# One latent trunk layer on one core: own tiles for each context head, two more weight pairs, and a new order of the opening

## The chip, the cores and the metric

The kernel runs on one core of one Trainium2 chip. The metric is the device time of one execution in microseconds; of several runs the median is taken. Matrix products are made on TensorE (PE), elementwise work on VectorE (DVE), ScalarE (ACT) and GpSimd (POOL); SyncE (SP) issues nearly all transfers.

## The reference, cut to what matters

One layer over 2048 latent rows (`x`) and 256 context rows (`ctx`), 1024 wide. The parts that the opening of the kernel computes:

```python
ada   = silu(c) @ w_ada + b_ada            # shifts and scales for x
ada_c = silu(c_ctx) @ w_ada + b_ada        # shifts and scales for the context
hc = modulate(rmsnorm(xc, norm_mix[l]), csh1, csc1)
logf_f, k_f, logf_b, k_b, vc = hgrn2_gates(hc @ w_in[l][:, :3 * w], lb_f, lb_b, first)
hf_c = advance_state(h0, k_f, vc, jnp.cumsum(logf_f, axis=2))
hb_c = advance_state(h0, flip_t(k_b), flip_t(vc), jnp.cumsum(flip_t(logf_b), axis=2))
h = modulate(rmsnorm(x, norm_mix[l]), sh1, sc1)
o, _, _ = token_mixers(h @ w_in[l], lb_f, lb_b, first, hf_c, hb_c, *mix_args)
x = x + g1 * (o @ w_out[l])
```

`hc @ w_in` has 3 x 512 columns: four heads with a forward gate, a backward gate and a value column block of 128 each, so 12 blocks. `hf_c` and `hb_c` are one 128 x 128 state per head and direction, from which the latent scans start. Then come a second normalisation, a gated MLP with a 3 x 3 convolution, and a last norm.

## The kernel before, in words

All large products are made as three products of split operands: `split` (L129) rounds an array to a high part on ScalarE (L131, a cast) and subtracts it to get the low part on VectorE or GpSimd (L132); `mm3` and `run_banks` multiply high by high, high by low and low by high into one PSUM bank. A *column* here is one block of 128 columns of `w_in` (its first column number is its key: 0 and 128 ... for the forward gates, 512 ... for the backward gates, 1024 ... for values, 2048 for the output gate of head 0). A *bank* is the product of one column with 256 context rows or with 512 rows of x: 24 matrix products.

**The opening**, L332 to L390, is written in a fixed order. `load_ada` fetches four 512-column groups of the conditioning weights. Groups 0, 2 and 3 are multiplied on TensorE (`ada_products`); group 1 is summed on VectorE (`ada_sums`, L290) and added up over the partitions by eight small products per sequence with a column of ones (`ada_ones`, L293). `ctx_mod` (L308) applies shift and scale to the context, block by block, and splits it; `ctx_products` (L323) starts the first column. `x_square` (L229) sums the squares of a tile of 128 rows on ScalarE, `rstd` makes the factors on GpSimd, `x_scale` (L234) multiplies a tile by them on VectorE (L238).

**The banks** behind it are the list `seq` (L1043 to L1047), an order written by hand in a string: `c` is the next of the 12 context banks, `g` a bank of head 0's output gate on x (the two share the column 2048), `v` and `q` its value and query banks, `s` and `t` banks of the gating unit. `run_banks` (L512) makes each bank, and before it fetches and splits the columns of the next two. A split column lies in one of two operand pairs (`w_free`, L209); it gives the pair back when its last bank is done. Raw columns come through three buffers.

Between banks `slot` steps two queues of background work. `bg_q` holds `x_start` (L406: normalise and transpose the first 1024 rows of x; `x_first` modulates and splits them, L243 and L132, into `xh` and `xl`; odd blocks get the low part on VectorE, even ones on GpSimd), then `misc`, then `x_second` (the other 1024 rows, to memory). `hg_q` holds `ctx_state` (L599) of each context head: seven level updates of the keys (L501) with products of totals (L508) on VectorE, four transposes, four products. The context heads share two sets of tiles in turn (`sets`, L638), so head h waits for the state of head h - 2 (L649).

A scheduler then orders the instructions on each engine, except in the fixed part and for those that are pinned.

Of the kernel before, what the change touches and what calls it, by code (L numbers as in the profile page):

```python
# [18 lines left out]
P = 128  # L19
# [64 lines left out]
def tile_trunk(ctx, tc, x, c, cx, c_ctx, w_ada, b_ada, norm_mix, norm_ffn, w_in, hg_norm, sgu_g, sgu_b,  # L84
# [104 lines left out]
    with es1:  # L189
# [18 lines left out]

        w_n, w_raw, w_free = [0], {}, [0, 1]  # L209

# [5 lines left out]
        def split_w(key, eng=None):  # L216
            if key not in w_raw:
                load_raw(key)
            raw, at = w_raw.pop(key), w_free.pop(0)
            hi = p1.tile([P, NK, P], F32R, tag=f"whi{at}", name="whi", align_bytes=AL)  # L220
            lo = p1.tile([P, NK, P], F32R, tag=f"wlo{at}", name="wlo", align_bytes=AL)
            w_n[0] += 1
            split(hi, lo, raw, eng or (V if w_n[0] < 8 or w_n[0] < 20 and w_n[0] % 2 else G))
            return hi, lo, at

        def x_sums():
            return pm.tile([P, 8], F32, tag="xss", name="xss", bufs=2)
# [6 lines left out]
        def x_scale(xs, ss, keep=pin):  # L234

            r = rstd(pm, ss[:, :len(xs)], len(xs), 1.0 / D, keep=keep)
            for i, xt in enumerate(xs):
                keep(V.tensor_scalar(out=xt, in0=xt, scalar1=r[:, i:i + 1], scalar2=None, op0=ALU.mult))  # L238

# [83 lines left out]
        def ctx_products(c, ks):  # L323
            hi, lo, _ = nxt[c, CTX]
            pj = opened[c, CTX]
            for k in ks:
                mm3(pj[:, :CTX], hi[:, k, :], lo[:, k, :], chl[:, k, :], cll[:, k, :], k == 0, False)

# [3 lines left out]
        with tc.manual_schedule():  # L332
# [33 lines left out]
            ada_rows(0, "ot")  # L366
            ada_sums(1, 0, 5)
            load_raw((2 * HW, CTX))
# [4 lines left out]
            ada_products(3, 1, 8)  # L373
            ctx_mod(0)
            ada_sums(1, 5, 8)
            for k in range(1, 4):
                ctx_mod(k)
                ada_sums(0, k - 1, k)
            nxt[HW, CTX] = split_w((HW, CTX), V)
            ss0 = x_sums()  # L380
            x_square(xg[:1], ss0, keep=lambda i: i)
            ada_rows(3, "ot")
            ada_ones(1, small, 256)
            ada_columns(3)
# [7 lines left out]
        xh = p1.tile([P, NK, TH], F32R, tag="xh", name="xh", align_bytes=AL)  # L392

# [12 lines left out]
        def x_start():  # L406
            xk = [pk.tile([P, 2, D], F32, tag="K", name="xk", bufs=2, align_bytes=AL) for i in range(2)]
            xs = [xk[i // 2][:, i % 2, :] for i in range(4)]
            ss, ss2 = ss0, x_sums()
            for q in range(2):  # L410
                x_square(xg[2 * q + 1:2 * q + 3], ss, 2 * q + 1)
                for i in range(2 * q, 2 * q + 2):
                    pin(ld(xs[i], x_rows[4 + i]))
                if q:
                    x_scale(xg, ss)
                yield 2.0
            for i, w in enumerate(x_first(0, xg)):
# [38 lines left out]
        def misc():  # L456

            for l in range(0, 8, 4):
                mf = pm.tile([P, 4, P], F32, tag="gu", name="mf", bufs=2)
                ld(mf, masks.rearrange("p (l j) -> p l j", j=P)[:, l:l + 4, :])  # L460
                V.tensor_copy(msk[:, l:l + 4, :], mf)
            yield 1.0
            wsr = pm.tile([P, NH, P], F32, tag="nt", name="wsr", bufs=2)
            ld(wsr, w_sp[0].rearrange("h p q -> p h q"))
# [47 lines left out]
        def run_banks(banks, peek=None):  # L512
# [3 lines left out]
            for i, (col, n0, n, sink, pre) in enumerate(banks):  # L516
                if pre is not None:
                    pre()
                up = list(dict.fromkeys(keys[i:] + tail))
                for key in up[:2]:  # L520
                    if key not in nxt:
                        nxt[key] = split_w(key)
# [4 lines left out]
                pj = opened.pop(keys[i], None)  # L527
                k0 = 0 if pj is None else 4
                pj = pj or bank("pj")
# [68 lines left out]

        def ctx_state(h, F, K, vt):  # L599
            tot = F  # L600
            for B in LV:
# [29 lines left out]
        def marked(g, what):  # L631
# [12 lines left out]
        for h in range(NH):  # L644
            F, K, vt = sets[h % 2]

            def pre(h=h):
                if h >= 2:
                    need(hg_q, ("ctx", h - 2))  # L649
                if h:  # L650
                    F, K, vt = sets[(h - 1) % 2]
                    hg_q.add(marked(ctx_state(h - 1, F, K, vt), ("ctx", h - 1)))
# [5 lines left out]
        def ctx_last():  # L658
            hg_q.add(marked(ctx_state(NH - 1, *sets[1]), ("ctx", NH - 1)))

# [1145 lines left out]
```

## Time and profile before

| | us |
|---|---|
| median of 3 runs | 2476.84 (2475.95 to 2477.19) |
| the profiled execution | 2477.96 |
| its span, first to last instruction | 2476.2 |
| TensorE busy (share of the span) | 2421.4 (98%) |
| VectorE, GpSimd, ScalarE busy | 1784.7 (72%), 1053.7 (43%), 968.2 (39%) |

The span is what the profile shows; the profiled execution's own time is 1.8 us longer and lies 1.1 us above the median. Times in the rows are counted from the start of the span. A row's bracket tells how long the engine was idle before it and what ended that.

### The profile page before, as it was taken

The page shows a single profiled execution, that of the slowest core. Times are in us where ns is not written, and L with a number is a line of the kernel's source. Part 1 is how long each engine was busy: PE and PEld are TensorE (multiplying, and loading weights), DVE is VectorE, ACT ScalarE, POOL GpSimd, SP SyncE. Part 2 cuts the span into 40 slices and gives each one's busy share as a digit, 9 for nine tenths or more (in the row PEclk, how much of TensorE's full clock was granted, in tenths as well). Part 3 has the DMA queues.
Part 4 walks back from the last instruction along what each step waited for, and adds up shares of the span by engine and source line. Part 5 has one row for each costly group of instructions (what it writes and reads, how often), then busy time and mean ns, then how long its engine had stood idle before and what let it go on. Part 6 is the DMA issues. An engine that isn't in the chain of part 4 may idle for free.

```text
span 2476.2 us, 32805 instructions
## 1 busy us (share of the span) xinstructions
PE 2421.4 (98%) x11859; PEld 2009.7 (81%) x11859; DVE 1784.7 (72%) x2374; ACT 968.2 (39%) x1614; POOL 1053.7 (43%) x866
## 2 busy tenths in 40 slices
PE   7899999999999999999999999999999999999998
PEld 4787888788888888788878888888878888888887
DVE  5766875645765866465699778759999993776876
ACT  3454334434344443244443333334333342432343
POOL 1344232332333433100588787887878770000002
PEclk9999999999999999999999999999999999999999
DMA  8365445573353422768932222472222239834645
GB/s 304 96 191 184 128 137 189 177 261 120 103 182 129 144 99 86 241 210 258 310 106 90 89 80 90 143 273 86 83 93 85 91 101 354 309 120 153 225 149 195
DMA packets 307854, 400.12 MB, mean 162 GB/s; under 512 B 33113, under 2 KB 216161, under 8 KB 304621
## 3 DMA queue, kind: packets, MB, share of 16 engines
q1 hardware_dynamic: 304404, 397.28, 48.3%
q8 instruction: 94, 1.54, 0.3%
q10 hardware_dynamic: 3289, 0.76, 0.1%
q14 instruction: 67, 0.55, 0.1%
HBM read 288.85 MB, written 109.13 MB: 161 GB/s over the span
## 4 chain that ended last, share of the span: by engine, by line
PE 37%; DVE 7%; issue 3%; POOL 2%; ACT 1%; DMA 1%; SPq 0%; POOLq 0%; ACTq 0%; DVEq 0%
PE up L65 23%; PE dn L65 14%; DVE dn L1373 3%; DVE edges L1378 1%; DVE gp L1454 1%; ACT dn L1370 1%; POOL Al L132 0%; DMA yd<-fl 0%; POOL ra L1665 0%; POOL rr L1666 0%; DVE keep L1448 0%; POOL raw L1191 0%; DVE keep L1464 0%; ACT Ah L131 0%; ACT cv L1392 0%
## 5 line engine op out<-in xcount | busy, mean ns | idle before, releaser
L1373 DVE SCALAR_TENSOR_TENSOR dn<-gp,taps,dn 128x1024 f32<-128x1024 f32 x352 | 448.6, 1281 | 21.1 <-ACT dn L1370 17.9
L65 PE MATMUL up<-yf,Ah 128*128 128x512 f32 x1232 | 393.5, 389 | 0.0
L65 PE MATMUL dn<-thl,mhl 128*128 128x512 f32 x1680 | 381.5, 389 | 1.2 <-ACT thl L131 1.2
L132 POOL TENSOR_TENSOR Al<-raw,Ah 128x512 fp32r<-128x512 f32 x264 | 343.0, 1308 | 89.5 <-ACT Ah L131 81.4
L65 PEld LDWEIGHTS dn<-thl,mhl 128*128 128x128 f32 x1680 | 315.0, 188 | 67.7 <-ACT thl L131 2.0
L65 PE MATMUL pj<-xh,whi 128*128 128x512 f32 x896 | 363.8, 406 | 0.0
L65 PE MATMUL pj<-xh,wlo 128*128 128x512 f32 x896 | 350.8, 392 | 1.2 <-DVE wlo L132 1.2
L65 PE MATMUL pj<-xl,whi 128*128 128x512 f32 x896 | 350.3, 391 | 1.2 <-POOL xl L132 1.0
L65 PE MATMUL up<-xah,Al 128*128 128x512 f32 x704 | 275.5, 391 | 3.4 <-POOL Al L132 3.1
L65 PE MATMUL up<-xah,Ah 128*128 128x512 f32 x704 | 274.6, 390 | 0.6 <-ACT Ah L131 0.6
L65 PEld LDWEIGHTS up<-yf,Ah 128*128 128x128 f32 x1232 | 231.2, 188 | 47.9
L131 ACT CAST Ah<-raw 128x512 fp32r<-128x512 f32 x264 | 160.6, 618 | 276.3 <-PE up L65 213.7
L132 POOL TENSOR_TENSOR wlo<-raw,whi 128x1024 fp32r<-128x1024 f32 x55 | 135.5, 2464 | 250.3 <-ACT whi L131 224.3
L65 PE MATMUL up<-xal,Ah 128*128 128x512 f32 x528 | 205.5, 389 | 0.0
L65 PE MATMUL up<-yf,Al 128*128 128x512 f32 x528 | 205.2, 389 | 0.0
L65 PEld LDWEIGHTS pj<-xh,wlo 128*128 128x128 f32 x896 | 168.3, 188 | 37.5 <-DVE wlo L132 1.7
L65 PEld LDWEIGHTS pj<-xh,whi 128*128 128x128 f32 x896 | 168.8, 188 | 32.8 <-issue 3.5
L65 PEld LDWEIGHTS pj<-xl,whi 128*128 128x128 f32 x896 | 168.9, 189 | 31.8 <-POOL xl L132 1.8
L65 PE MATMUL dn<-wo,o 128*128 128x512 f32 x768 | 182.9, 394 | 1.8 <-DVE nt L706 0.9
L65 PEld LDWEIGHTS dn<-wo,o 128*128 128x128 f32 x768 | 141.9, 188 | 31.7 <-issue 1.1
L65 PEld LDWEIGHTS up<-xah,Al 128*128 128x128 f32 x704 | 132.1, 188 | 36.0 <-POOL Al L132 8.6
L1665 POOL TENSOR_SCALAR ra<-ss 128x1 f32<-128x1 f32 x8 | 5.3, 662 | 359.8 <-ACT jk L1657 359.8
(317 smaller groups left out, 4186.9 us busy)
## 6 DMA issues: line engine op xcount, KB each, us to landing
raw<-in_w_up_dram SPq DMA_DIRECT2D x88, 512.0 KB, 4.5
mr<-m SPq DMA_DIRECT2D x85, 512.0 KB, 5.3
raw<-in_w_in_dram SPq DMA_DIRECT2D x68, 512.0 KB, 4.3
sT<-wd SPq DMA_DIRECT2D x88, 256.0 KB, 4.4
raw<-in_w_ada_dram SPq DMA_DIRECT2D x32, 512.0 KB, 3.9
yf<-yd SPq DMA_DIRECT2D x14, 1024.0 KB
m<-cv SPq DMA_DIRECT2D x22, 544.0 KB, 2.7
raw<-in_w_down_dram SPq DMA_DIRECT2D x22, 512.0 KB, 3.8
```

The lines of the kernel that those rows point to most:

```text
L65: return self.engine.matmul(out, lhsT, rhs, **kw)
L131: keep(S.copy(hi, raw))
L132: (eng or G).tensor_sub(lo, raw, hi.bitcast(F32))
L1370: S.activation(cr, gt[:, 0:RH, 0:GW], AF.Identity, bias=cvb[:, f:f + 1], scale=taps[:, f:f + 1])
L1373: V.scalar_tensor_tensor(out=cr, in0=gt[:, t // 3:t // 3 + RH, t % 3:t % 3 + GW], scalar=taps[:, t * NF + f:t * NF + f + 1], in1=cr, op0=A ...
L1378: V.scalar_tensor_tensor(out=e[:, 0, :], in0=gt[:, 1, t % 3:t % 3 + GW], scalar=taps[:, t * NF + f:t * NF + f + 1], in1=e[:, 0, :], op0=AL ...
L1454: V.tensor_add(g_rows(hh, f + c, n2), quad(p, kind), quad(add, kind))
L1665: G.tensor_scalar(out=a, in0=ss, scalar1=plus, scalar2=None, op0=ALU.add)
```

## The change

- Each context head gets its own tiles for gates, keys and values (`sets`), so no bank waits for an earlier head's state; `ctx_state` first yields until x's first 1024 rows are done (`x0b`).
- Two more operand pairs, each used once, lie in the second half of `xh`, which is free until x's rows 512 to 1023 are split into it. `xh` is allocated earlier for that, inside the fixed part. The first bank now asks for up to four columns.
- All sums of group 1 stand between the context blocks, ahead of the last four blocks; the first column is finished in the fixed part; the third column is split there too.
- x's squares are taken sooner, inside the fixed part. In `x_scale` of four tiles, two of the four are scaled on ScalarE.
- The low part of the eighth split goes to VectorE; the masks' conversion is pinned behind their loads.
- The order of the banks: seven context banks, `g`, four context banks, `g`, the last context bank, then `v v q q s s s s t t t t`.

```diff
-        w_n, w_raw, w_free = [0], {}, [0, 1]
+        class Rows:
+            def __init__(self, ap):
+                self.ap = ap
+            def __getitem__(self, at):
+                k = at[1]
+                return self.ap[:, k // 4, (k % 4) * P:(k % 4) * P + P]
+
+        w_n, w_raw, w_free = [0], {}, [0, 1, 2, 3]
...
-            split(hi, lo, raw, eng or (V if w_n[0] < 8 or w_n[0] < 20 and w_n[0] % 2 else G))
-            return hi, lo, at
+            if at < 2:
...
+                split(hi, lo, raw, eng or (V if w_n[0] < 9 or w_n[0] < 20 and w_n[0] % 2 else G))
+                return hi, lo, at
+            hi, lo = (xh[:, k:k + 2, 512:] for k in (4 * at - 8, 4 * at - 6))
+            split(hi, lo, raw.rearrange("p (a b) c -> p a (b c)", a=2), eng or V, pin if at > 2 else lambda i: i)
+            return Rows(hi), Rows(lo), at
...
-                keep(V.tensor_scalar(out=xt, in0=xt, scalar1=r[:, i:i + 1], scalar2=None, op0=ALU.mult))
+                if i % 2 and len(xs) == 4:
+                    keep(S.activation(xt, xt, AF.Copy, scale=r[:, i:i + 1]))
+                else:
+                    keep(V.tensor_scalar(out=xt, in0=xt, scalar1=r[:, i:i + 1], scalar2=None, op0=ALU.mult))
...
-            ada_sums(1, 0, 5)
+            ada_sums(1, 0, 8)
...
-            ctx_mod(0)
-            ada_sums(1, 5, 8)
-            for k in range(1, 4):
+            for k in range(4):
                 ctx_mod(k)
-                ada_sums(0, k - 1, k)
+                ada_sums(0, max(0, 2 * k - 1), 2 * k + 1)
             nxt[HW, CTX] = split_w((HW, CTX), V)
+            ada_sums(0, 7, 8)
             ss0 = x_sums()
             x_square(xg[:1], ss0, keep=lambda i: i)
             ada_rows(3, "ot")
+            x_square(xg[1:2], ss0, 1, keep=lambda i: i)
...
                 ctx_mod(k)
-            ada_sums(0, 3, 8)
+                ctx_products(0, (k,))
             ada_ones(0, small, 288)
+            xh = p1.tile([P, NK, TH], F32R, tag="xh", name="xh", align_bytes=AL)
+            nxt[2 * HW, CTX] = split_w((2 * HW, CTX), V)
+            x_square(xg[2:3], ss0, 2, keep=lambda i: i)
+            x_square(xg[3:4], ss0, 3, keep=lambda i: i)
...
-                for key in up[:2]:
-                    if key not in nxt:
+                for key in up[:2 if w_n[0] > 3 else 4]:
+                    if key not in nxt and w_free:
                         nxt[key] = split_w(key)
...
-                    w_free.append(nxt.pop(keys[i])[2])
+                    at = nxt.pop(keys[i])[2]
+                    if at < 2:
+                        w_free.append(at)
...
         def ctx_state(h, F, K, vt):
+            for i in range(60):
+                if "x0b" not in done:
+                    yield 1.0
...
-        sets = [(cS[:, 0:2, :], cS[:, 2:4, :], view(cb, 0, [[1, CTX]])),
-                (view(cf, 0, [[CTX, 2], [1, CTX]]), view(cf, 2 * CTX, [[CTX, 2], [1, CTX]]), view(cb, CTX, [[1, CTX]]))]
+        c2, c3 = (ph.tile([P, 4, CTX], F32, tag=t, name="c" + t, bufs=2) for t in ("vt", "sgt"))
+        sets = [(t[:, 0:2, :], t[:, 2:4, :]) for t in (cS, view(cf, 0, [[CTX, 4], [1, CTX]]), c2, c3)]
+        sets = [(*kf, view(cb, h * CTX, [[1, CTX]])) for h, kf in enumerate(sets)]
...
-        for item in "c c c c c c g c g v c v q c q s c s s c s t c t t t".split():
+        for item in "c c c c c c c g c c c c g c v v q q s s s s t t t t".split():
```

Three places show how the built order moves. In them `xfl` is a modulated block, `xl` its low part, `wlo` a column's low part (in the change the third and fourth column's lie in `xh`), `cl` the context's low part, `xg` and `xk` tiles of x, `cS`, `cf`, `cvt` the context heads' gates and keys, `tot` products of totals.

VectorE, from the last context block on. Before:

```order
L319 TENSOR_TENSOR cl<-xfl,ch 128x256
L290 SCALAR_TENSOR_TENSOR acc<-wa,cs_75,acc 128x512 x2
L132 TENSOR_TENSOR wlo<-raw,whi 128x1024
L290 SCALAR_TENSOR_TENSOR acc<-wa,cs_75,acc 128x512 x3
L501 TENSOR_TENSOR cS<-cS 128x128x2
L508 TENSOR_TENSOR tot<-cS 128x256
L301 TENSOR_TENSOR s_72<-sc,bc 128x4
```

and now:

```order
L336 TENSOR_TENSOR cl<-xfl,ch 128x256
L318 TENSOR_TENSOR s_72<-sc,bc 128x4
L132 TENSOR_TENSOR xh<-raw,xh 128x2x512 x2
L255 TENSOR_SCALAR xg<-xg,rs_411 128x1024 x2
L522 TENSOR_TENSOR cS<-cS 128x128x2
L260 TENSOR_SCALAR xfl<-mi,a_71,s_72 128x512 x2
L132 TENSOR_TENSOR wlo<-raw,whi 128x1024 x2
```

The sums are gone from here, and the step `s_72`, which reads the small sums of TensorE, stands ahead of the third column's low part.

VectorE, at the low part that the first x bank needs (before: the one right behind the sixth `xfl`; now: the one behind the `xk` scalings). Before:

```order
L501 TENSOR_TENSOR cS<-cS,tot 128x2x2x64
L508 TENSOR_TENSOR tot<-tot 128x4
L243 TENSOR_SCALAR xfl<-mi,a_71,s_72 128x512
L132 TENSOR_TENSOR wlo<-raw,whi 128x1024
L243 TENSOR_SCALAR xfl<-mi,a_71,s_72 128x512
L132 TENSOR_TENSOR xl<-xfl,xh 128x512
L501 TENSOR_TENSOR cf<-cf 128x128x2
```

and now:

```order
L260 TENSOR_SCALAR xfl<-mi,a_71,s_72 128x512 x2
L522 TENSOR_TENSOR cS<-cS,tot 128x16x2x8
L529 TENSOR_TENSOR tot<-tot 128x32
L522 TENSOR_TENSOR cS<-cS,tot 128x8x2x16
L529 TENSOR_TENSOR tot<-tot 128x16
L522 TENSOR_TENSOR cS<-cS,tot 128x4x2x32
L132 TENSOR_TENSOR xl<-xfl,xh 128x512
L255 TENSOR_SCALAR xk<-xk,rs_662 128x1024 x2
L132 TENSOR_TENSOR wlo<-raw,whi 128x1024
```

That low part stood among x's first blocks and stands now behind all eight of them, behind most of head 0's updates and behind the scaling of the second four tiles.

GpSimd, from x's first low parts on. Before:

```order
L132 TENSOR_TENSOR xl<-xfl,xh 128x512 x3
L132 TENSOR_TENSOR wlo<-raw,whi 128x1024
L132 TENSOR_TENSOR xl<-xfl,xh 128x512
L124 TENSOR_SCALAR rs<-xss 128x4
L126 TENSOR_TENSOR rs_685<-rs,mhalf 128x4
```

and now:

```order
L132 TENSOR_TENSOR xl<-xfl,xh 128x512 x4
L124 TENSOR_SCALAR rs<-xss 128x4
L126 TENSOR_TENSOR rs_662<-rs,mhalf 128x4
L132 TENSOR_TENSOR xl<-xfl,xh 128x512 x2
L132 TENSOR_TENSOR wlo<-raw,whi 128x1024
L132 TENSOR_TENSOR xl<-xfl,xh 128x512 x2
L132 TENSOR_TENSOR wlo<-raw,whi 128x1024 x2
```

No column's low part is left among x's first blocks; three stand now between and behind the second blocks, for columns 9, 11 and 13.

## Rows read from the trace of the kernel before

**Rows 1.** The page: its first line, and TensorE's busy time.
```profile
span 2476.2 us, 32805 instructions
...
PE 2421.4 (98%) x11859; PEld 2009.7 (81%) x11859; DVE 1784.7 (72%) x2374; ACT 968.2 (39%) x1614; POOL 1053.7 (43%) x866
```

**Rows 2.** Busy time by stretch: us, PE, PEld, DVE, ACT, POOL, clock, DMA, GB/s.
```profile
55.00:59.00 4.00, 3.75 (x19) 3.48 (x20) 4.00 (x5) 1.41 (x3) 0.69 (x1) 0.57 0.26 75
78.00:83.00 5.00, 4.94 (x26) 4.63 (x27) 3.52 (x5) 0.62 (x1) 0.14 (x1) 0.66 0.00 0
```

**Rows 3.** TensorE's timeline, first context products: start, us, instruction, idle before.
```profile
40.14 0.39 PE L65 MATMUL pj<-ch,whi 128*128 128x256 f32 x1
...
48.35 0.39 PE L65 MATMUL pj<-ch,wlo 128*128 128x256 f32 x1 [0.76 <-DVE wlo L132]
...
50.73 0.95 PE L65 MATMUL sc<-ones,acc 128*128 128x2 f32 x8
51.53 0.36 PE L65 MATMUL pj<-ch,whi 128*128 128x256 f32 x1
```

**Rows 4.** TensorE's timeline, transposes of x and the first x bank.
```profile
60.32 1.03 PE L69 MATMUL mi<-ident,xg 128*128 128x128 f32 x8
61.12 0.36 PE L65 MATMUL pj<-ch,wlo 128*128 128x256 f32 x1
...
63.83 1.03 PE L69 MATMUL mi<-ident,xg 128*128 128x128 f32 x8
...
70.86 0.50 PE L65 MATMUL pj<-xh,wlo 128*128 128x512 f32 x1 [0.90 <-DVE wlo L132]
71.19 0.39 PE L65 MATMUL pj<-xh,whi 128*128 128x512 f32 x1
...
72.35 0.40 PE L65 MATMUL pj<-xh,wlo 128*128 128x512 f32 x1
...
78.06 0.30 PE L69 MATMUL mi<-ident,xk 128*128 128x128 f32 x1 [1.92 <-DVE xk L238]
```

**Rows 5.** TensorE's timeline, the second x bank and later waits.
```profile
98.40 0.50 PE L65 MATMUL pj<-xh,wlo 128*128 128x512 f32 x1 [0.26 <-DVE wlo L132]
...
151.78 0.63 PE L69 MATMUL mi<-ident,cS 128*128 128x128 f32 x4 [0.82 <-DVE xfl L243]
...
201.99 1.13 PE L65 MATMUL mi<-wsT,nt 128*128 128x128 f32 x8 [0.94 <-DVE xfl L243]
```

**Rows 6.** VectorE's timeline.
```profile
39.52 0.16 DVE L301 TENSOR_TENSOR s<-sc,bc 128x4 f32<-128x4 f32 x1 [1.18 <-PE sc L65]
...
47.07 1.23 DVE L132 TENSOR_TENSOR wlo<-raw,whi 128x1024 fp32r<-128x1024 f32 x1
48.22 2.32 DVE L290 SCALAR_TENSOR_TENSOR acc<-wa,cs,acc 128x512 f32<-128x512 f32 x3
...
52.76 2.74 DVE L238 TENSOR_SCALAR xg<-xg,rs 128x1024 f32<-128x1024 f32 x4 [0.55 <-POOL rs L126]
...
56.55 1.52 DVE L243 TENSOR_SCALAR xfl<-mi,a,s 128x512 f32<-128x512 f32 x2
...
59.12 0.68 DVE L132 TENSOR_TENSOR xl<-xfl,xh 128x512 fp32r<-128x512 f32 x1
...
115.80 2.61 DVE L501 TENSOR_TENSOR cS<-cS,tot 128x256 f32<-128x256 f32 x1
...
118.54 0.43 DVE L501 TENSOR_TENSOR cS<-cS,tot 128x256 f32<-128x256 f32 x1
```

**Rows 7.** ScalarE's timeline, the third column's cast.
```profile
46.00 1.04 ACT L131 CAST whi<-raw 128x1024 fp32r<-128x1024 f32 x1 [1.51 <-PE pj L65]
```

**Rows 8.** GpSimd's timeline, low parts.
```profile
62.73 1.30 POOL L132 TENSOR_TENSOR xl<-xfl,xh 128x512 fp32r<-128x512 f32 x1 [1.58 <-ACT xh L131]
...
69.68 3.38 POOL L132 TENSOR_TENSOR wlo<-raw,whi 128x1024 fp32r<-128x1024 f32 x1
...
115.67 2.46 POOL L132 TENSOR_TENSOR wlo<-raw,whi 128x1024 fp32r<-128x1024 f32 x1 [1.23 <-ACT whi L131]
```

More of the change, by code (lines that the diff above doesn't have):

```diff
@@ L219, in split_w @@
             raw, at = w_raw.pop(key), w_free.pop(0)
-            hi = p1.tile([P, NK, P], F32R, tag=f"whi{at}", name="whi", align_bytes=AL)
-            lo = p1.tile([P, NK, P], F32R, tag=f"wlo{at}", name="wlo", align_bytes=AL)
             w_n[0] += 1
-            split(hi, lo, raw, eng or (V if w_n[0] < 8 or w_n[0] < 20 and w_n[0] % 2 else G))
-            return hi, lo, at
+            if at < 2:
+                hi = p1.tile([P, NK, P], F32R, tag=f"whi{at}", name="whi", align_bytes=AL)
+                lo = p1.tile([P, NK, P], F32R, tag=f"wlo{at}", name="wlo", align_bytes=AL)
+                split(hi, lo, raw, eng or (V if w_n[0] < 9 or w_n[0] < 20 and w_n[0] % 2 else G))
[3 more added lines that the diff above has]
+            return Rows(hi), Rows(lo), at
         def x_sums():
@@ L326, in ctx_products @@
             for k in ks:
-                mm3(pj[:, :CTX], hi[:, k, :], lo[:, k, :], chl[:, k, :], cll[:, k, :], k == 0, False)
+                mm3(pj[:, :CTX], hi[:, k, :], lo[:, k, :], chl[:, k, :], cll[:, k, :], k == 0, k == NK - 1)
         xg = [ph.tile([P, D], F32, tag=t, name="xg", bufs=2) for t in ("vt", "vt", "sgt", "sgt")]
@@ L388, in tile_trunk @@
                 ctx_mod(k)
-            ada_sums(0, 3, 8)
+                ctx_products(0, (k,))
             ada_ones(0, small, 288)
+            xh = p1.tile([P, NK, TH], F32R, tag="xh", name="xh", align_bytes=AL)
+            nxt[2 * HW, CTX] = split_w((2 * HW, CTX), V)
+            x_square(xg[2:3], ss0, 2, keep=lambda i: i)
+            x_square(xg[3:4], ss0, 3, keep=lambda i: i)
         xl = p1.tile([P, NK, TH], F32R, tag="xl", name="xl", align_bytes=AL)
-        xh = p1.tile([P, NK, TH], F32R, tag="xh", name="xh", align_bytes=AL)
         def x_first(g0, xs):
@@ L409, in x_start @@
             ss, ss2 = ss0, x_sums()
[L410 to L416, printed above, removed]
+            x_scale(xg, ss)
+            for i in range(4):
+                pin(ld(xs[i], x_rows[4 + i]))
+                if i % 2:
+                    yield 2.0
             for i, w in enumerate(x_first(0, xg)):
@@ L456, in misc @@
         def misc():
+            mfs = []
             for l in range(0, 8, 4):
@@ L460, in misc @@
                 ld(mf, masks.rearrange("p (l j) -> p l j", j=P)[:, l:l + 4, :])
-                V.tensor_copy(msk[:, l:l + 4, :], mf)
+                mfs.append(mf)
             yield 1.0
+            for l in range(2):
+                pin(V.tensor_copy(msk[:, 4 * l:4 * l + 4, :], mfs[l]))
             wsr = pm.tile([P, NH, P], F32, tag="nt", name="wsr", bufs=2)
@@ L527, in run_banks @@
                 pj = opened.pop(keys[i], None)
-                k0 = 0 if pj is None else 4
+                k0 = 0 if pj is None else NK
                 pj = pj or bank("pj")
@@ L644, in tile_trunk @@
         for h in range(NH):
-            F, K, vt = sets[h % 2]
+            F, K, vt = sets[h]
             def pre(h=h):
-                if h >= 2:
-                    need(hg_q, ("ctx", h - 2))
                 if h:
-                    F, K, vt = sets[(h - 1) % 2]
+                    F, K, vt = sets[h - 1]
                     hg_q.add(marked(ctx_state(h - 1, F, K, vt), ("ctx", h - 1)))
@@ L658, in ctx_last @@
         def ctx_last():
-            hg_q.add(marked(ctx_state(NH - 1, *sets[1]), ("ctx", NH - 1)))
+            hg_q.add(marked(ctx_state(NH - 1, *sets[NH - 1]), ("ctx", NH - 1)))
         qb_d = [dr.tile([P, TH], F32, name=f"qb{h}") for h in range(NH)]
```

## The prediction

> **What bounds the kernel.** I read the page first. Of a span of 2476.2 us TensorE is busy 2421.4 [rows 1], and the change adds and drops no matrix product, so all it can give back is time in which TensorE waits or runs at its half clock. That time I looked up in TensorE's timeline and waits up to 320 us, then in the timelines of the engines that end those waits.
>
> From 40.14 us, the first product of the context [rows 3], to 98.40, the low part of the second x bank [rows 5], 58.26 us pass. How much work stands there? A product of 256 columns takes 0.12 us (22 of them between 61.12 and 63.83), one of 512 columns 0.23 (71.19 to 72.35 is five), a transpose 0.10 (eight from 60.32 to 61.12) [rows 4], the eight small conditioning sums 0.80 [rows 3]. The order of before has 168, 48 and 80 of these in that stretch, the sums, and 0.9 of small products: 20.2 + 11.0 + 8.0 + 1.7 = 40.9 us. So 17.4 us are lost there. After 98.40 TensorE's timeline shows no wait up to 151.78; then come five up to 201.99, together 3.4 us (the first and the last stand in [rows 5]).
>
> What ends the waits before 98.40 is VectorE. The third weight column waits for its operand pair (ScalarE's cast starts at 46.00 after TensorE gives the pair back [rows 7]) and for its low part, until 48.35 [rows 3]. The transposes of x wait for VectorE's scaling, 1.92 us at 78.06, and the first x bank waits for its low part at 70.86 [rows 4]. Two of the stretches behind such holes run at the low clock: 0.57 and 0.66 of full speed on the mean of 55 to 59 and 78 to 83 [rows 2]. In the second that loses 5 x 0.34 = 1.7 us.
>
> **The change part by part.** *Conditioning sums.* Two more sums of 0.77 us (2.32 for three [rows 6]) come ahead of the step at 39.52, which waits 1.18 us for TensorE [rows 6]. So 1.5 us go into 1.2 of slack; ops that follow each other closely save some 0.1, and I take a start of the context products at 40.3, 0.15 late.
>
> *Two more pairs.* The third column no longer waits for a pair: its cast can follow ScalarE's fourth late modulation at about 44.6. Its low part, though, now stands on VectorE behind the step that reads the small sums from TensorE, and those come after the first key's last product. TensorE reaches them at 46.1, they take 0.95 [rows 3], then the step, then 1.23 for the low part [rows 6]: about 48.45. The work up to there is 50 products and the sums, 6.8 us, so 40.3 + 6.8 = 47.1, and 1.35 is waited. From there on the fourth to seventh columns find their parts ready, where before TensorE crept from 52 to 58: only 0.15 and 0.85 us of waits are left, the latter for the seventh column's low part.
>
> *Squares sooner, two of four scalings on ScalarE.* The factors are there at about 49.4, before the transposes need them. ScalarE is not on the path (39% of the span [rows 1]); four more ops of the size of a cast (1.04 [rows 7]) cost nothing while its wait is for VectorE.
>
> *The first x bank.* Here the lead ends. Its low part is put behind everything that VectorE does for x's first half and behind the scaling of the second. From 47.15 that is: six low parts at 1.15, eight modulations at 0.76, four of x's low parts at 0.60, four scalings at 0.68, and seven level updates of context head 0 with five products of totals, 3.6 us in all (singles by [rows 6], less the 0.08 by which starts run ahead of ends). Together 21.7. It waits some 1.35 us for data. And GpSimd's four low parts of x (1.30 each [rows 8]) hold it up: the level update at 115.80 took 2.61 us instead of 0.43 [rows 6] because it began behind GpSimd's low part of 115.67 and ran on just after that one's end [rows 8]. Laying the two engines' orders side by side I find holds of 1.35, 1.25, 0.75 and 1.15, so 4.5 us. 47.15 + 21.7 + 1.35 + 4.5 = 74.7; I use 74.8. TensorE has come to that bank at 67.4, finds its high part at 70.95, does two products and waits to 74.8: 7.0 us lost. Then I add one fall of the clock as in the second of [rows 2], 1.7.
>
> The Trainium skill, page "SBUF — State Buffer", section "SBUF: two separate sides", calls the port pair of VectorE and GpSimd an exclusive lock: who starts first has it for the whole instruction. If each of the four holds were a whole GpSimd low part, they would sum to 5.2, and the forecast would rise by 0.7 us.
>
> *Four context columns between the two x banks.* Both x banks use one column, which keeps one of the two lasting pairs, and the two new ones are used once. So columns 8 to 11 share one pair, and each must wait for TensorE to end the one before: cast 1.04 [rows 7], low part 1.23 on VectorE or 2.46 on GpSimd [rows 6, 8]. Of that I take off what TensorE has beside it. Column 9: 1.04 + 2.46 less 0.8 of transposes and 0.24 of high products is 2.4. Column 10: its low part follows two modulations and ends 3.15 after the key before, against 2.0 of other work: 1.1. Column 11: 3.55 less 2.1: 1.5. Later 0.2. Sum 5.2.
>
> *Sum.* Up to the third product of head 0's value bank the new order has 288 products of 256 columns, 50 of 512, 76 transposes and the small work: 34.6 + 11.5 + 7.6 + 1.7 = 55.4. Before has done as much at 98.40 + (55.4 - 40.9) = 112.9. After: 40.3 + 55.4 + 1.35 + 0.15 + 0.85 + 7.0 + 1.7 + 5.2 = 111.95. Gain 1.0. Behind it, no context bank stands among the gating banks and four table switches go from ScalarE, so I take half of the first two of the five later waits, 0.9 of 1.8; between nothing and all of 3.4. All in all -1.9. What comes after 200 us has nearly the same order, and TensorE is the bound there, so it moves along. The profiled execution took 2477.96 and would take 2476.1; the median of the runs shown is 1.1 below it, so **2474.9 us**.
>
> **The rivals.** *VectorE keeps up.* For it: the holds are placed by hand, and GpSimd may run its low parts while VectorE waits for data. Without the 4.5 us the first x bank is ready at 70.3: 2474.9 - 4.5 = 2470.4. Against it: from 55 to 59 VectorE had no idle time at all [rows 2]. *The one pair is the new bound (slower).* From 82 to 100 us each of columns 9 to 11 depends on cast and low part. GpSimd's low part took 3.38 instead of 2.46 where VectorE got in its way [rows 8]; three times 0.92 is 2.8. If each of the three waits then passes the 1.92 us after which the clock fell at 78.06 [rows 4], three falls of 1.7 come on top: +7.9, 2482.8. It decides as soon as these waits reach about 2 us. Against it: behind the wait of 0.90 at 70.86 the products follow each other at full clock, 0.23 apart [rows 4].
>
> By the exclusive lock of that page of the Trainium skill GpSimd could be held for as long as a whole VectorE low part, 3 x 1.23 = 3.7, and this case would end at 2483.7. The row of 3.38 speaks for less.
>
> *The change doesn't do what it says*: the states are not all behind x's columns. In the order head 0's seven updates still stand among them. That is in the sum (3.6 us); were they really gone, the first x bank would come as much sooner. No chance is left for this one by itself.
>
> **How the numbers follow.** Forecast 0.62, VectorE keeps up 0.28, one pair 0.10. 0.2% of the median, about what a measurement of this kernel can tell from no change, is 5.0 us: under 2471.9 is faster, over 2481.8 slower. The first rival is nearly all faster, the second slower, the forecast the same but for the chance that the later waits go too. So 0.28, 0.62, 0.10. The range takes in the first rival with 1.7 more of the later waits, 2468.7, and upward the stretched low parts, one more fall and no gain in the later waits (2.8 + 1.7 + 0.9), 2480.3, and leaves the second rival out.
>
> **What would show it.** Right: the third column's low part near 48.4; TensorE without a wait over 1 us from 49 to 67, then some 7 us of wait ended by the cast and by VectorE's low part; three waits of 1 to 2.5 us for low parts between 82 and 101, none before. Wrong: the first x bank's low part before 72, a clock under full after 85 more than once, or waits of the later stretch that grow.

## The result and the profile after

| | before | changed |
|---|---|---|
| median | 2477.79 us (6 runs, 2475.95 to 2480.92) | 2486.77 us (6 runs, 2483.49 to 2492.42) |
| ratio, 95% interval | | 1.0036 [1.0021, 1.0051] |
| the profiled execution, its span | 2477.96, 2476.2 us | 2483.49, 2481.7 us |

The change costs 9 us. That is over the 5.0 us that count here as slower, above the forecast of 2474.9 and above the range (2468.7 to 2480.3). The profiled execution of the changed kernel is the fastest of its six; the others lie up to 8.9 us higher, the highest at a mean granted clock of 0.993 instead of 0.997.

The page, to be held against [rows 1]: TensorE's busy time is 2.3 us less and the span 5.5 us more. The number of products is the same (x11859), so no work was added; TensorE stood still for 7.8 us longer.

```profile
span 2481.7 us, 32803 instructions
...
PE 2419.1 (97%) x11859; PEld 2010.5 (81%) x11859; DVE 1776.4 (72%) x2371; ACT 967.1 (39%) x1614; POOL 1047.7 (42%) x865
```

TensorE's timeline up to the second x bank (start, us, instruction, idle time before it and what ended that):

```profile
38.52 0.38 PE L69 MATMUL sc<-ident,rows 2*128 2x2 f32 x4 [2.64 <-DVE s L318]
...
48.48 0.50 PE L65 MATMUL pj<-ch,xh 128*128 128x256 f32 x2 [1.04 <-DVE xh L132]
...
65.77 0.39 PE L65 MATMUL pj<-ch,wlo 128*128 128x256 f32 x1 [0.31 <-DVE wlo L132]
...
72.18 0.50 PE L65 MATMUL pj<-xh,whi 128*128 128x512 f32 x1 [3.29 <-ACT whi L131]
...
76.58 0.80 PE L65 MATMUL pj<-xh,wlo 128*128 128x512 f32 x1 [3.67 <-DVE wlo L132]
...
91.69 0.39 PE L65 MATMUL pj<-ch,wlo 128*128 128x256 f32 x1 [1.93 <-POOL wlo L132]
...
97.85 0.38 PE L65 MATMUL pj<-ch,wlo 128*128 128x256 f32 x1 [1.04 <-DVE wlo L132]
...
104.26 0.38 PE L65 MATMUL pj<-ch,wlo 128*128 128x256 f32 x1 [1.30 <-POOL wlo L132]
```

These rows answer to [rows 3, 4 and 5]. The third column's low part is there at 48.48, no wait over 1 us follows until 69, then come 3.29 and 3.67 us at the first x bank, and then the three waits for the shared pair. All of that was forecast, but for the last of the three, which ends at 104.26 instead of before 101. The later rows were not:

```profile
164.87 0.63 PE L69 MATMUL mi<-ident,xk 128*128 128x128 f32 x4 [1.44 <-DVE tot L529]
...
206.33 0.33 PE L69 MATMUL mi<-ident,xk 128*128 128x128 f32 x1 [1.95 <-DVE xk L255]
...
251.92 2.19 PE L65 MATMUL sc<-Q,K 128*128 128x128 f32 x16 [2.17 <-ACT K L604]
256.44 0.66 PE L69 MATMUL mi<-ident,vv 128*128 128x128 f32 x4 [1.63 <-ACT vv L611]
...
302.18 1.16 PE L65 MATMUL mi<-vt,kt 128*128 128x128 f32 x8 [1.63 <-DVE nt L723]
```

In the kernel before, the wait for `xk` at 196.65 and the two larger ones near those at 252 and 302:

```profile
196.65 1.42 PE L69 MATMUL mi<-ident,xk 128*128 128x128 f32 x11 [0.27 <-DVE xk L238]
...
247.44 2.19 PE L65 MATMUL sc<-Q,K 128*128 128x128 f32 x16 [1.79 <-ACT K L581]
...
298.56 0.66 PE L69 MATMUL mi<-ident,gv 128*128 128x128 f32 x4 [0.65 <-DVE nt L698]
```

From 113 to 345 us TensorE waits 9.9 us where it waited 6.9 before (seven waits now, five of them shown; nine before). Up to 215 us that is 4.1 against 3.4, behind it 5.8 against 3.5: most of the growth lies behind 215 us. The lag behind the kernel before is some 2.4 us at the value bank of head 0 (its third product at 115.34, against the 112.9 that the prediction reckons for the kernel before), 2.7 at the last context head's products (215.97 against 213.23) and 5.2 at 339; the end is 5.5 late.

Four stretches of the changed kernel by windows (us, PE, PEld, DVE, ACT, POOL, clock, DMA, GB/s), to be held against [rows 2]:

```profile
36.00:44.00 8.00, 5.48 (x35) 5.50 (x35) 6.28 (x14) 4.54 (x9) 0.00 (x0) 0.79 1.05 385
48.00:52.00 4.00, 3.52 (x18) 3.52 (x19) 2.98 (x4) 3.26 (x6) 1.50 (x2) 0.63 0.52 152
72.00:76.00 4.00, 0.73 (x2) 0.30 (x2) 3.63 (x8) 2.15 (x3) 1.77 (x3) 0.61 0.00 0
76.00:80.00 4.00, 3.42 (x9) 2.70 (x10) 3.00 (x7) 1.91 (x5) 0.00 (x0) 0.53 0.44 131
```

Each of the waits that end at 38.52 and at 48.48, and the pair at 72.18 and 76.58, has a fall of the clock with it: three, where one was forecast. (A mean such as 0.53 says that the stretch ran almost wholly at the lower of the clock's two levels, 1.2 instead of 2.4 GHz.) From 80 us to the end of TensorE's work the granted clock was 1.00 in this execution.

### The profile page after: what moved, and what is told of

It is laid out like the page before. It is cut to its first block, busy times and chain, and to the rows that moved or that the text cites. A ratio compares the mean times of both kernels' runs of the same rounds, so it can differ in the third digit from the quotient of the medians.

```text
span 2481.7 us, 32803 instructions
## 1 busy us (share of the span) xinstructions
PE 2419.1 (97%) x11859; PEld 2010.5 (81%) x11859; DVE 1776.4 (72%) x2371; ACT 967.1 (39%) x1614; POOL 1047.7 (42%) x865
## 5 line engine op out<-in xcount | busy, mean ns | idle before, releaser
L65 PEld LDWEIGHTS up<-xah,Ah 128*128 128x128 f32 x704 | 132.1, 188 | 28.7 <-ACT Ah L131 1.8
```

The source lines that it names most:

```text
L65: return self.engine.matmul(out, lhsT, rhs, **kw)
```

## Experiments

Two theories stood at the start. The early theory: the loss arises between 49 and 113 us and is handed on one to one. The late theory: the order behind 150 us decides, and an early gain is waited away there. Every kernel ran five rounds, those of one group on one chip beside the kernel before, whose medians there were 2477.35 (runs 1 to 4), 2477.6 (5 to 8) and 2478.06 (9 to 12). One context bank is `c`, a half of head 0's gate bank over x is `g`.

### First group: which part costs

**Run 1**, level updates in program order:

```diff
-            V.tensor_mul(o, o, t)
+            pin(V.tensor_mul(o, o, t))
```

> The changed kernel, with the level updates of the context states held in program order, so that on VectorE head 0's stand behind all of x's columns (in the changed kernel they stand among the first half's, 61.4 to 73.1 us). Early theory (the loss arises between 49 and 113 us, at the first x bank's low part and in the four columns on one pair, and is handed on one to one): the updates that leave VectorE's queue there took 6.4 us with GpSimd's holds, so the first x bank's low part ends near 71 instead of 76.6; TensorE's 7 us of wait fall to some 2, and the end comes about 5 us sooner: 2481.8. Late theory (the order behind 150 us decides, an early gain is waited away at later rows): no more than 1 us sooner, 2486. If the holds by GpSimd and not the updates were the cause, 2 us or less.

Measured: 2488.11 us (1.0045 [1.0032, 1.0057]). The early half did what was expected, though less of it: the waits between 55 and 80 fell from 7.3 to 4.4 us and the first transposes of rows 512 to 1023 came at 79.22 instead of 81.13. All of it was lost again: head 3's totals, which now stand late as well, made TensorE wait at 226:

```profile
226.34 1.09 PE L69 MATMUL mi<-ident,csgt 128*128 128x128 f32 x4 [4.60 <-DVE tot L529]
```

**Run 2**, the order of banks:

```diff
-        for item in "c c c c c c c g c c c c g c v v q q s s s s t t t t".split():
+        for item in "c c c c c c c c c c g c g c v v q q s s s s t t t t".split():
```

> The changed kernel with another order of banks: ten context columns ahead of the first x bank instead of seven, and one context column between the two x banks instead of four. Early theory: TensorE has three columns (11.6 us) of other work before it needs the first x bank's low part, so that wait of 7 us goes, and of the three waits for a shared pair (1.9, 1.0, 1.3 us) at most one is left; in exchange it may wait 1 to 3 us for x's second half. 5 to 9 us sooner: 2478 to 2482. Late theory: the value bank comes sooner by as much, but the waits at 165, 206, 252, 256 and 302 us stay or grow, 2485 to 2487.

Measured: 2483.09 us (1.0025 [1.0016, 1.0034]), 3.7 sooner than the changed kernel. One half of the expectation was wrong in an instructive way: the wait did not go but stayed in eighth place, at a context column this time.

```profile
70.49 0.48 PE L65 MATMUL pj<-ch,whi 128*128 128x256 f32 x1 [3.27 <-ACT whi L131]
...
74.73 0.58 PE L65 MATMUL pj<-ch,wlo 128*128 128x256 f32 x1 [3.55 <-DVE wlo L132]
...
205.11 0.30 PE L69 MATMUL mi<-ident,xk 128*128 128x128 f32 x1 [3.15 <-DVE xk L255]
```

So it belongs to the eighth pair that VectorE and ScalarE make, whatever it is for. What went are the waits for the shared pair: from 75 to 125 us there is none, and the transposes of the first half of head 0's value bank (a mark behind all twelve context columns and both x banks in either order; called the value mark below) came at 117.47 instead of 124.57, 7.1 us sooner. At the last context head's transposes 3.2 us of that were left (210.20 against 213.45), at 435 us 1.1.

**Run 3**, low parts of the columns between the x banks:

```diff
-                split(hi, lo, raw, eng or (V if w_n[0] < 9 or w_n[0] < 20 and w_n[0] % 2 else G))
+                split(hi, lo, raw, eng or (V if w_n[0] < 13 or w_n[0] < 20 and w_n[0] % 2 else G))
```

> The changed kernel, with the two GpSimd low parts of the context columns between the x banks made by VectorE (1.22 instead of 2.36 us each). Early theory: the waits of 1.93 and 1.30 us fall to about 0.8 and 0.2, the end comes 2 us sooner (2484.8), if VectorE's low parts of x are not pushed back by as much. If VectorE is the bound there, nothing is gained (2486.8), since 2.4 us more stand in its queue ahead of the second x bank. Late theory: nothing is gained either, though the value bank comes 2 us sooner.

Measured: 2487.54 us (1.0034 [1.0022, 1.0047]), nothing gained that five runs could tell. In place of the waits of 1.93, 1.04 and 1.30 us stand two, 1.85 and 1.09: for the first column VectorE is as late as GpSimd was.

**Run 4**, the order of banks of the kernel before, all else as changed:

```diff
-        for item in "c c c c c c c g c c c c g c v v q q s s s s t t t t".split():
+        for item in "c c c c c c g c g v c v c q c q s c s s c s t c t t t".split():
```

> The changed kernel with the order of banks of the kernel before: six context columns, an x bank, one column, the second x bank, and the other columns among the value, query and gating banks. All other parts of the change stay. Early theory: TensorE comes to the first x bank a column (3.9 us) sooner and waits some 10 us there, but no column waits for a shared pair behind it (4.7 us less), so about 1 us is gained: 2485.5. Late theory: the order behind 113 us is again that of the kernel before, the 3 us of later waits that the change added go, 2482 to 2483; more than that (2478) if the order of banks is all that cost time.

Measured: 2478.08 us (1.0002 [0.9993, 1.0010]). This is the last case of the expectation: no different from the kernel before. With the old order the time is gone, so the order of the banks costs it; pairs, squares, scalings and sums together neither cost nor give anything that can be told (some 2 us, by the interval).

### Second group: what in the order costs

The background work that transforms x's second 1024 rows (`x_second`) goes in four quarters of 256 rows. Its planned times here are the kernel's own count of TensorE's work at which it writes a piece into the program. They are no times of the chip.

**Run 5**, run 2 with shorter pauses in it:

```diff
-                yield 6.0
+                yield 3.0
                 ss = x_sums()
                 x_square(xs, ss)
                 x_scale(xs, ss)
-                yield 6.0
+                yield 3.0
```

> The order of the second run (ten context columns, x bank, one column, x bank), and in the background work that transforms x's second half the two pauses after the loads and after the scaling cut from 6 to 3 planned us, so that its last quarter stands some 17 planned us sooner in the program (142.8 instead of 159.7; 155.4 in the changed kernel, 150.9 in the kernel before). Place theory (a later second x bank pushes x's second half to just ahead of the gating banks, which need all of it, and the early gain is waited away there: 6.6 us of waits between 125 and 206 us in the second run): most of these waits go, 3 to 5 us sooner than the second run, 2478 to 2480. Rival (VectorE is short of time there because no context column stands among the later banks): the waits stay under other names, at most 1 us sooner, 2482 to 2483.

Measured: 2481.00 us (1.0013 [1.0004, 1.0021]), 2.1 sooner than run 2, between the two. The waits did not go, they moved: 0.9 to 1.0 us at 121, 142 and 162 and 3.79 at 187.59, always for the scaling of the next quarter. So its place in the program alone is not what limits it. The 2.1 us go with rows that the expectation didn't name: from 215 to 345 us TensorE waits 1.5 us, 6.3 in run 2, and none of the three waits at 252, 256 and 302 is there.

**Run 6**, x banks early, the other five context columns behind them:

```diff
-        for item in "c c c c c c c g c c c c g c v v q q s s s s t t t t".split():
+        for item in "c c c c c c g c g c c c c c v v q q s s s s t t t t".split():
```

> The changed kernel with the x banks where the kernel before has them (behind six columns, one column between), and the other five context columns all together behind them, ahead of the value bank. Place theory: x's second half stands where it did within 2.3 planned us (153.2 against 150.9), the early part runs as in the fourth run, so 2478 to 2480. Rival (the columns missing among the later banks are what costs): the waits behind 150 us stay as in the changed kernel or in the second run, 4 to 6 us of them, 2482 to 2484.

Measured: 2486.16 us (1.0032 [1.0019, 1.0044]), against the place theory and over its rival's 2482 to 2484. At the value mark it led the changed kernel by 4.4 us (120.15 against 124.57). Then came one wait that took more than all of it:

```profile
180.92 0.60 PE L69 MATMUL mi<-ident,xk 128*128 128x128 f32 x4
...
199.52 0.45 PE L69 MATMUL mi<-ident,xk 128*128 128x128 f32 x1 [6.37 <-DVE xk L255]
```

**Run 7**, only the first x bank one place sooner:

```diff
-        for item in "c c c c c c c g c c c c g c v v q q s s s s t t t t".split():
+        for item in "c c c c c c g c c c c c g c v v q q s s s s t t t t".split():
```

> The changed kernel with only the first x bank one place sooner (behind six columns; five columns between the banks). In the second run the eighth bank waited 7 us though it was a context column, so the wait belongs to the eighth low part in VectorE's queue (ready near 76), not to the x bank. If so, the x bank in seventh place gives TensorE 5.5 us of work ahead of it and the wait falls from 7 to 1 or 2 us; the end comes 3 to 5 us sooner, 2482 to 2484, less what x's second half takes back near 206 us. If the x bank itself is what is late, TensorE waits as long one place sooner, and nothing is gained: 2487.

Measured: 2481.88 us (1.0016 [1.0007, 1.0025]), 4.9 sooner, as expected if the wait belongs to the eighth pair: from 55 to 80 us 3.2 us of waits instead of 7.3, none at the eighth cast, and its low part 0.95 late.

**Run 8**, the kernel before with the new order alone:

```diff
-        for item in "c c c c c c g c g v c v c q c q s c s s c s t c t t t".split():
+        for item in "c c c c c c c g c c c c g c v v q q s s s s t t t t".split():
...
-                    if key not in nxt:
+                    if key not in nxt and w_free:
```

> The kernel before with the new order of banks alone: two operand pairs, context heads 0 and 2 sharing tiles, squares, scalings and conditioning sums as before. If the order is all that costs and the other parts do nothing, it takes as long as the changed kernel, 2486 to 2488. If the other parts soften the order (pairs, tiles of their own), it is slower: 2489 to 2494. If they are what costs, 2478 to 2480.

Measured: 2487.86 us (1.0039 [1.0026, 1.0052]), as the changed kernel. (The `and w_free` lets a fetch wait while both pairs are taken.) With run 4 the four corners are complete: old order 2477.6 and 2478.1 (old and new rest), new order 2487.9 and 2486.8.

### Third group: the chain that takes the lead back

Waits for `xk` of 1.95 to 6.37 us stand at 187 to 210 us in the changed kernel and in every run so far but run 4, which has the old order. What lies behind them? In the kernel before, from the last transposes of the third quarter to the first of the fourth (TensorE; SP issues the loads; ScalarE squares, GpSimd makes the factor, VectorE scales):

```profile
182.49 0.60 PE L69 MATMUL mi<-ident,xk 128*128 128x128 f32 x4
...
183.00 0.34 SPq L435 DMA_DIRECT2D xk<-in_x_dram  x1
...
188.47 0.42 SPq L435 DMA_DIRECT2D xk<-in_x_dram  x1
...
193.36 0.19 ACT L232 ACTIVATION_READ_ACCUMULATOR xjk<-xk 128x1 f32 x1
...
193.70 0.19 POOL L124 TENSOR_SCALAR rs<-xss 128x2 f32<-128x2 f32 x1 [0.45 <-ACT xjk L232]
...
195.17 1.42 DVE L238 TENSOR_SCALAR xk<-xk,rs 128x1024 f32<-128x1024 f32 x2 [1.79 <-POOL rs L126]
...
196.07 0.30 PE L69 MATMUL mi<-ident,xk 128*128 128x128 f32 x1
```

and in the changed kernel:

```profile
190.53 0.66 PE L69 MATMUL mi<-ident,xk 128*128 128x128 f32 x4 [0.68 <-DVE nt L723]
...
193.35 0.46 SPq L453 DMA_DIRECT2D xk<-in_x_dram  x1
...
195.77 0.42 SPq L453 DMA_DIRECT2D xk<-in_x_dram  x1
...
199.18 1.05 ACT L131 CAST whi<-raw 128x1024 fp32r<-128x1024 f32 x1 [3.89 <-PE pj L65]
...
200.62 1.04 ACT L246 ACTIVATE xjk<-xk 128x1024 bf16<-128x1024 f32 x1
...
202.66 1.30 POOL L699 TENSOR_TENSOR nt<-nt,gu 128x512 f32<-128x512 f32 x1
202.76 0.18 ACT L246 ACTIVATION_READ_ACCUMULATOR xjk<-xk 128x1 f32 x1
...
204.05 0.19 POOL L124 TENSOR_SCALAR rs<-xss 128x2 f32<-128x2 f32 x1
...
205.52 1.42 DVE L255 TENSOR_SCALAR xk<-xk,rs 128x1024 f32<-128x1024 f32 x2 [6.04 <-POOL rs L126]
```

A quarter's rows lie in one tile. So the next load waits for the last transposes, and load, squares, factor and scalings follow each other: 13.0 us from the end of one row to the start of the other before (196.07 - 183.09), 15.1 in the changed kernel (206.33 - 191.19), 18.0 in run 6 (199.52 - 181.52). Without the wait at its end, that stretch is TensorE's other work between the two: 13.0 us before, where it waits for nothing there and so has no slack; 13.2 in the changed kernel; 11.6 in run 6; and 10.7 in run 2, whose chain takes 13.8. So this cover runs out in two ways. In runs 2 and 6 TensorE has less other work beside the chain. In the changed kernel it has as much, but the chain is 2.2 us longer. The second load lands at 199.6 (3.8 us after its issue), and the squares end 3.4 us later, for the cast of a weight column and another step stand ahead of them on ScalarE; before it was 1.3 us (192.3 to 193.55). The factor starts 1.1 us behind the squares, held by `nt` on GpSimd; before 0.15. (The second load itself is issued 0.8 us sooner.)

**Run 9** gives the changed kernel a second tile, where the context's rows were:

```diff
+            two = [pk.tile([P, 2, D], F32, tag="K", name="xk2", bufs=2, align_bytes=AL)]
...
+                if g == 2:
+                    two.append(pk.tile([P, 2, D], F32, tag="F", name="xk2", align_bytes=AL))
+                xk[g] = two[g // 2 % 2]
...
+                    if g + 2 < NCH and k in (0, 4):
+                        (scaled if k else load)(g + 2)
```

(`load` issues a quarter's loads, `scaled` takes squares, factor and scalings; the pauses between the pieces became 4.0 each. So three things change together, the tile, the earlier loads and scalings, and the pauses; they weren't tried one by one.)

> The changed kernel, with a second tile for x's second half (where the context's rows were, free once the twelve columns are done), so that a quarter is loaded, squared and scaled while the quarter before is being transposed. Chain theory (in one tile load, squares, factor and scalings of a quarter follow each other, and TensorE, whose order is fixed, has too little other work beside the last one because the second x bank came later): the wait of 1.95 us at 206 goes, the one of 1.44 at 165 probably too, 2 to 3 us sooner, 2484 to 2485. Rival (VectorE has too much to do between 150 and 206 us): the same time is waited at other rows, 2486 to 2487.

Measured: 2483.75 us (1.0025 [1.0015, 1.0034]), 3.0 sooner. The wait at 206 went, and those at 252 and 256, but from 113 to 215 us still 4.9 us are waited, at other rows (1.28 for ScalarE's `ckt`, 1.46 for `xfl`, 1.78 for `nt`). Its profiled execution is the slowest of its nine. For this order both theories hold in part.

**Run 10**, second tile and the order of run 2:

> The same second tile with the order of the second run (ten context columns, x bank, column, x bank), which led the changed kernel by 7 us at 117 us and had 3 of it left at 210. Chain theory: of its 7.4 us of waits between 125 and 206 us at least 4 go, and what is saved is handed on, 2477 to 2479. Rival (VectorE short of time): 2482 to 2483 as in the second run.

Measured: 2471.55 us (0.9978 [0.9969, 0.9988]), 11.5 sooner than run 2, more than expected, and 0.22% faster than the kernel before. The scaling of the last quarter (VectorE) is now done 5.6 us ahead of its first transposes (TensorE, 184.19), and from 113 to 215 us 1.1 us is waited, 0.25 of it behind 127, where run 2 waits 7.4:

```profile
176.68 1.89 DVE L255 TENSOR_SCALAR xk<-xk,rs 128x1024 f32<-128x1024 f32 x2 [0.82 <-POOL rs L126]
```
```profile
184.19 0.60 PE L69 MATMUL mi<-ident,xk 128*128 128x128 f32 x4
...
194.35 0.63 PE L69 MATMUL mi<-ident,xk 128*128 128x128 f32 x4 [0.25 <-DVE xfl L260]
```

The lead over the kernel before, by rows that stand behind the same work, is 4.9 us at 353, 6.3 at 451 and 5.8 at 2048: here it is handed on. How much of the 0.22% the second tile would give with the old order of banks wasn't tried.

**Run 11**, run 10 with head 0's updates, and only these, in program order:

```diff
-                level_update(K, CTX, B, tot, True)
+                level_update(K, CTX, B, tot, True, pin if h == 0 else lambda i: i)
```

> As the run before it, and head 0's level updates (its alone) held behind x's columns on VectorE, which the first run did for all heads: there the eighth low part came sooner, but head 3's totals were late by 4.6 us at 226. If the updates are what makes the eighth low part late: the two waits of 3.3 and 3.6 us at 70 and 75 us shrink by 2 to 4 us together, 2474 to 2476. If the cast on ScalarE, behind x's high parts, is: at most 1 us, 2477 to 2478.

Measured: 2471.87 us (0.9973 [0.9964, 0.9983]). In the profile the waits of 3.28 and 3.46 us became 2.63 (seventh cast), 0.81 and 0.23, and the span is 1.8 us shorter (2468.6 against 2470.4), but the medians of runs 10 and 11 can't be told apart. The updates do make the eighth low part late; what the end has from that stays open.

**Run 12**, second tile and the order of run 7:

> The second tile with the order of the seventh run (first x bank in seventh place, five columns, second x bank). Chain theory: its wait of 1.95 us at 205 goes, 2479 to 2480, and what is left against the kernel before are the five columns on one pair (some 5 us of waits between 84 and 105). Rival: 2482.

Measured: 2479.64 us (1.0012 [1.0002, 1.0021]), 2.2 sooner than run 7, as expected. Against run 10 it lacks 8.1 us. Both have the second tile, and what differs is the place of the x banks. Between 80 and 113 us its rows show 6.6 us of waits where run 10 has none, the larger of them for the shared pair (run 10 for its part waits 6.7 us at 72 and 76, run 12 3.2 between 55 and 80):

```profile
91.05 0.39 PE L65 MATMUL pj<-ch,wlo 128*128 128x256 f32 x1 [1.93 <-POOL wlo L132]
...
95.01 0.39 PE L65 MATMUL pj<-ch,whi 128*128 128x256 f32 x1 [1.06 <-ACT whi L131]
...
102.64 0.39 PE L65 MATMUL pj<-ch,wlo 128*128 128x256 f32 x1 [1.25 <-POOL wlo L132]
```

At the value mark it is 3.9 us behind run 10 (122.69 against 118.76), at 233 us 6.8. So about half of the 8.1 arises early, the other half later. Of the later half, run 12 shows a wait of 1.94 us at 164.01 and a granted clock of 0.61 from 164 to 168; the rest I did not take apart.

Runs 2, 9 and 10 with the changed kernel answer the question of the two theories:

| us | one tile | second tile |
|---|---|---|
| the change's order | 2486.77 | 2483.75 (run 9) |
| x banks behind ten columns | 2483.09 (run 2) | 2471.55 (run 10) |

The place of the x banks is worth 3.7 us with one tile and 12.2 with two; at the value mark it is 7.1 and 8.6 (127.31 against 118.76; run 9 has one fall of the clock more on the way there, 0.66 from 92 to 97 us, which is 1.7). The kernels before of the three sets differ by up to 0.7 us in their medians, which is small against this. The loss in the early stretch is real. With one tile half of an early gain is waited away beside the chain of x's second half and most of the rest behind it (the profiled execution of run 2 leads by 7.1 us at 117, 3.2 at 210, 1.1 at 435); with two it is handed on, and at least 3.6 us more come later.

## Why the prediction was wrong

- **The start and the third column** (forecast: products at 40.3, low part at 48.45). The low part came at 48.48. The products started 1.5 us sooner than forecast, and TensorE lost that again at a lower clock: from 38.82 to 48.48 it took 9.7 us for 6.8 of work and 1.04 of wait. That the two cancel is luck. The early start goes with the clock too: from 28 to 34 us it was granted 1.00 here and 0.50 in the profiled execution of before; in run 10, with 0.57 from 27 to 35, the products start at 40.08.
- **The first x bank** (7.0 us of wait, ready at 74.8). 3.29 + 3.67 us were waited. It was ready at 76.58, and TensorE came 1.5 us later than forecast; in runs 2 and 3, whose clock didn't fall behind 48 us, the same low part was ready at 74.73 and 75.07. The reason given, what stands ahead of it in VectorE's order, is borne out by runs 1 and 11, where the waits shrink with head 0's updates moved; runs 2 and 7 show it is the eighth pair's, not the x bank's.
- **One pair for four columns** (5.2 us). 4.9 were waited. The term was right.
- **The sum up to the value bank** was too small on the clock. It had one fall of 1.7 us. The profile shows three: 1.8 us up to 48.48; 1.5 between 48.48 and 68.9 (20.4 us instead of the 18.9 that runs 2 and 3 needed without a fall); 1.6 behind 76.58 (13 products in 4.55 us instead of 2.99). The value bank's third product came at 115.34 instead of 111.95: falls 3.2 more, start and waits 2.9 less, and 3.1 of work that took longer than my count of it, which stays unexplained. The gain of 1.0 over the 112.9 of before was a loss of 2.4. (The low part at 98.40 in [rows 5] is not the second x bank's, as the prediction has it, but that of the value bank behind it: both x banks share one column. It moves the count by one product.)
- **"What comes after 200 us has nearly the same order, and TensorE is the bound there, so it moves along", and "half of the first two of the five later waits" gained: this is the step that failed most.** The waits from 113 to 345 us grew by 3.0 instead of shrinking by 0.9, which the prediction names as a sign that it is wrong. Up to 215 us they grew by 0.7: the wait at 206 is 1.7 longer, and smaller ones went. The scaled rows of the last quarter depend on a chain as long as TensorE's work beside it. In the trace of before this showed as a wait of only 0.27 us at 196.65 for `xk`, which I passed over. The other 2.4 stand at 252, 256 and 302 us, where the orders differ in details: at 256 TensorE transposes `vv` 4.5 us behind the products at 251.92 (before: 6.1 behind 247.44) and waits 1.63, because ScalarE's copy of `vv` stands behind a copy of keys that waits for GpSimd. Runs 2, 5 and 6 show the lead taken back at the chain, run 10 that it is kept with the second tile.
- **The median.** I put it 1.2 us below the profiled execution, by the runs shown of before. It lies 3.3 above: this execution is the fastest of its six.

In numbers: 3.4 us up to 115, 3.9 in the later waits and 0.1 unplaced make the 7.4 by which the profiled execution missed its 2476.1; 4.5 are the median's place. VectorE did not keep up: the first rival asked for the bank at 70.3, it was ready at 76.58. The slower rival named the right place, the shared pair, but its price (low parts stretched to 3.38) did not come: those of GpSimd took 2.35 and 2.37.

The late waits at 252, 256 and 302 us were not tried one by one, so their cause stays open beyond the order of the banks. In run 4 with the old order two of the three are absent, in run 5 all three, and in runs 9, 10 and 12 the first two; the third stays there at 1.6.

## What to carry to other kernels

When a change moves the work of a busy engine forward, follow the chains that run beside it (load, squares, factor, scaling in one tile) to their next meeting point: a chain that had just enough of that engine's other work beside it can be the next bound, and a wait of a few tenths there (0.27 us here) can be its sign. Test a reordering with and without that chain relieved; measured alone, the two were worth 3.7 and 3.0 us, together 15.2. In a sum, count falls of the clock on both sides or on neither.

## What was not expected of the hardware

The clock does not fall behind every wait of one length. The same step, the copy of `vv`, was waited for 1.87 us in run 4 and 1.86 us in the kernel before:

```profile
448.88 0.80 PE L69 MATMUL mi<-ident,vv 128*128 128x128 f32 x4 [1.87 <-ACT vv L611]
```
```profile
448.00:452.00 4.00, 3.12 (x10) 2.58 (x11) 3.63 (x6) 1.93 (x4) 0.00 (x0) 0.66 0.36 136
```
```profile
450.00:454.00 4.00, 2.86 (x15) 2.46 (x16) 3.94 (x6) 2.20 (x5) 0.00 (x0) 1.00 0.35 133
```

The first two fences are run 4 (timeline, windows), the third is the kernel before around its 451.14. In run 4 the clock fell to 0.66 and 1.6 of its 2.3 us of lead were gone by 460; in the kernel before it stayed at 1.00. The changed kernel and run 2 show it too: both wait 1.04 us for the third column's low part, at 48.48 and 48.29, and the clock is 0.63 from 48 to 52 in the one and 1.00 from 47 to 52 in the other. So two profiled executions can differ by such falls, some 1.7 us each here, behind the same wait for the same step. The six runs of the changed kernel spread over 8.9 us, and their mean granted clock goes from 0.997 at 2483.49 and 2484.16 us to 0.993 at 2492.42; 0.004 of the span would be 10 us (an estimate). The kernel before spreads over 5.0 in six runs, but over 8.9 in the 28 of the third group, so that the changed kernel has more falls than it is not shown.

In run 6 the scaling that TensorE waited 6.37 us for took 3.48 us instead of 1.42:

```profile
196.55 3.48 DVE L255 TENSOR_SCALAR xk<-xk,rs 128x1024 f32<-128x1024 f32 x2 [5.49 <-POOL rs L126]
```

GpSimd had begun a low part of 2.34 us at 196.49, just ahead of it. The excess of 2.06 us, a third of the wait, is nearly that whole low part. This fits the exclusive lock that the Trainium skill describes (page "SBUF — State Buffer", section "SBUF: two separate sides"), and it is the same picture as the level update of 2.61 us in [rows 6].
